# A fourth seven-product unit, low parts on GpSimd, and small transfers on SP's queue in an encoder block's gate/up stage

## Chip, core and metric

The kernel runs on one core of one Trainium2 chip. The metric is device microseconds of one execution, lower is better; the median of three runs is shown, and one more execution was profiled.

## The reference

One pre-norm encoder layer on a sequence of 256 rows, width 2048, everything in float32:

```
x = x + mix(rms_norm(x)) @ w_out            # four mixers: GLA, FNet, Hyena, short convolution
x = x + cross_attention(rms_norm(x), rms_norm(mem), w_xq, w_xkv, w_xo)
gate, up = split(rms_norm(x) @ w_gate_up)   # w_gate_up: 2048 x (2 * 5632)
x = x + (silu(gate) * up) @ w_down
return rms_norm(x)
```

Only the third line and the start of the fourth are touched by the change. The inputs that matter there are the 2048 x 11264 weight matrix, and 256 rows of normalised activations.

## The kernel before

**Precision by splitting.** TensorE multiplies float32r, which keeps fewer bits than float32. Each weight tile `raw` is therefore split into a high part `wh` (a cast on ScalarE, line 156) and a low part `wl = raw - wh` (a subtraction on VectorE, line 157); activations are split alike. A product is three matmuls (lines 495 to 497): high by high, high by low, low by high. One of these products is 128 rows of the sequence by 128 of the contraction by 512 columns.

**The weight stream.** Weights are laid out in HBM in the order of their use, in slabs of 16 blocks of 128 x 128 (1 MB, 128 x 2048). `Stream.raw` loads a slab on SP's queue (line 136) into one of three buffers, four in this stage; `Stream.make` splits a slab in parts of 1024 columns ahead of use, as long as `wh`/`wl` buffers are free: five parts in this stage.

**Plain slabs and units.** A plain slab of gate/up is two contraction tiles by two blocks of 512 columns; with two halves of the rows that is eight products. `seven(slab)` tells the slabs that are done as a *unit* instead: a Strassen-like form with seven products. For it the four blocks of the slab are first used as they are or replaced, in place, by sums and differences (line 189), and four parts are split: 512, 1024, 1024 and 1024 columns. The matching sums of activations are formed once, by `left()` (line 966), ahead of the first unit. The seven products of a unit partly go to four extra PSUM banks (p1, p5, p7, p6), into which all units of a pass add up.

**The loop.** `gate_up` (line 956) makes eleven passes over j. Each computes a block of 512 columns of gate and one of up: eight slabs i = 0 to 7. In pass 0 slab 5 is a unit, in passes 1 to 10 slabs 1, 3 and 5 (`sevens`, line 53). After the last unit `combine` (line 995) folds the four extra banks into SBUF tiles, starting with a copy of p1 (line 1000); the passes alternate between the two PSUM pools, so that the extra banks of one pass are the main ones of the next. After slab 7 `finish` (line 1009) adds the main banks, applies silu and the product, transposes the result on VectorE in blocks of 32 (line 525, into `u`) and stores it to HBM in `hidden` (line 530).

**Background work.** `combine`, `finish`, `turn`, `fetch` and `left` are generators that a planner (`Background`) steps between matmuls, by its own count of the work that VectorE owes (`bg.dve`). `turn` (line 1067) transposes the 16 residual tiles on VectorE, stores them to `xrows` and loads them back in row order (lines 1077, 1081); `fetch` (line 932) loads hidden tiles back and splits them for the next stage. In the stage described here, all of these transfers are issued on GpSimd's queue. The framework settles each engine's order by readiness, except where `keep_place` ties an instruction to the one before it; on its queue, each engine then issues strictly in that order.

**GpSimd's work.** Besides DMA issues it has a few memsets and one select at the kernel's start; it computes nothing in this stage.

Of the kernel before, what the change touches and what calls it, by code (L numbers as in the profile page):

```python
# [13 lines left out]
F32 = mybir.dt.float32  # L14
# [4 lines left out]
ALU = mybir.AluOpType  # L19
# [3 lines left out]
P = 128  # L23
R = 256
# [26 lines left out]
GU = 16 * (40 + 16 + 16 + 32 + 16)  # L51

def sevens(j):

    return (1, 3, 5) if j else (5,)


FORMED = 6
# [20 lines left out]
DOWN = GU // 16 + 16 * DFF // 1024  # L79
# [6 lines left out]
def seven(slab):  # L86

    j, i = divmod(slab - GU // 16, 8)
    return slab in UNITS if slab >= DOWN else j >= 0 and i in sevens(j)
# [22 lines left out]
class Stream:  # L112
# [34 lines left out]
                return pool  # L147
        return None

    def split(self, pool, at, r, edges):  # L150

        nc = self.nc
        wh, wl = (pool.tile([P, 1088], F32R, name=t, tag=t) for t in ("wh", "wl"))
        wh, wl = wh[:, at:at + 1024], wl[:, at:at + 1024]
        for a, b in zip(edges, edges[1:]):
            nc.scalar.copy(wh[:, a:b], r[:, a:b])  # L156
            nc.vector.tensor_tensor(out=wl[:, a:b], in0=r[:, a:b], in1=wh[:, a:b].bitcast(F32), op=ALU.subtract)  # L157
        self.bg.dve(edges[-1], len(edges) - 1)
        self.items.append((pool, wh, wl))

    def make(self):

        nc, (slab, part) = self.nc, self.todo
        n = 16 * slab + 8 * part
        if n >= NBLK - HELD:
            parts = [(self.places.pop(0)) for _ in range(2)]
            r = self.raw(slab)[:, part * 1024:part * 1024 + 1024]
            for a, (wh, wl) in zip((0, 512), parts):
                nc.scalar.copy(wh, r[:, a:a + 512])
                nc.vector.tensor_tensor(out=wl, in0=r[:, a:a + 512], in1=wh.bitcast(F32), op=ALU.subtract)  # L170
            self.bg.dve(1024, 2)
            self.items.append((None, parts))
            self.todo = (slab + part, 1 - part)
            return True
        pool = self.free(slab)
        if pool is None:
            return False
        raw = self.raw(slab)
        at = 48 if any(a <= n < b for a, b in ROWS) else 8
        r = raw[:, part % 2 * 1024:part % 2 * 1024 + 1024]  # L180
        if not seven(slab):
            mark = len(nc.cur_bb.bb.instructions)
            self.split(pool, at, r, [0, 256, 512, 1024] if n == 0 else [0, 512, 1024] if n == 8 else [0, 1024])
            if DOWN <= slab < DOWN + 2 * AHEAD:
                self.keep(mark)
            self.todo = (slab + part, 1 - part)
            return True
        mark = len(nc.cur_bb.bb.instructions)
        op = lambda out, a, b, what=ALU.subtract: nc.vector.tensor_tensor(out=out, in0=a, in1=b, op=what)  # L189
        self.split(pool, at, r, [0, 512] if part == 0 else [0, 1024])  # L190
        b11, b12, b22, b21 = (raw[:, a:a + 512] for a in range(0, 2048, 512))
        if part == 0:
            blk = raw.rearrange("p (b c) -> p b c", b=4)
            op(r.rearrange("p (b c) -> p b c", b=2), blk[:, 0:3:2, :], blk[:, 1:2, :].to_broadcast([P, 2, 512]))
            self.bg.dve(1024)
        elif part == 1:
            op(b22, b22, b11, ALU.add)
            op(b21, b21, b22)
            self.bg.dve(1024, 2)
        self.keep(mark)  # L200
        self.todo = (slab + part // 3, (part + 1) % 4)
        return True
# [87 lines left out]
class Block:  # L290
# [229 lines left out]
    def store_turned(self, to, u, src, keep=False):  # L520

        nc = self.nc
        self.bg.dve(src.shape[1])
        mark = self.mark()
        nc.vector.transpose(u, src)  # L525
        if keep:
            self.keep_place(mark)
        to = to.rearrange("(b f) t -> f b t", f=32)
        for a in range(4):
            nc.gpsimd.dma_start(to[:, :, 32 * a:32 * a + 32],  # L530
                                u[32 * a:32 * a + 32, :].rearrange("f (b t) -> f b t", t=32))


    def run(self):
# [237 lines left out]
    def attention(self):  # L772
        tc, nc, act, st = self.tc, self.nc, self.act, self.st
        with tc.tile_pool(name="atp", bufs=1) as atp, tc.tile_pool(name="kp", bufs=1) as kp, \
# [24 lines left out]
            def load_kv():  # L799
# [12 lines left out]
                for _ in range(5):  # L812
                    fetch()
# [118 lines left out]
    def fetch(self, f, ks, ahead, pause, form=None):  # L932

        m = {}
        for n in range(len(ks) + ahead):
            if n < len(ks):
                k = ks[n]
                while len(self.stored) <= k // 4:
                    yield
                m[k] = self.tmp()  # L940
                self.nc.gpsimd.dma_start(m[k], self.ff[k * P:(k + 1) * P, :])  # L941
            if n >= ahead:
                i = ks[n - ahead]
                if i >= PLAIN:
                    if i % 2:
                        form(i - 1, m.pop(i - 1), m.pop(i))
                        self.have += 2
                        yield 3.0
                    continue
                mark = self.mark()  # L950
                self.split(f[i], m.pop(i))
                self.keep_place(mark)
                self.have += 1
                yield pause

    def gate_up(self, sw, gp, f):

        nc, st = self.nc, self.st
# [6 lines left out]

        def left():

            for i in (5, 1, 3):
                t = [self.tmp() for _ in range(2)]
                for x, k in zip(t, (2 * i, 2 * i + 1)):  # L970
                    nc.scalar.activation(x, self.resk(k), AF.Copy, scale=self.gvec(V_NG + 32, k))
                (a11, a21), (a12, a22) = ((x[:, 0:P], x[:, P:R]) for x in t)
                s = gp.tile([P, 512], F32, name="u", tag="u", bufs=2)
                s1, s2, s3, s4 = (s[:, a:a + P] for a in range(0, 512, P))
                self.stt(s1, a21, -1.0, a22, ALU.mult, ALU.subtract)
                self.stt(s2, s1, -1.0, a11, ALU.mult, ALU.subtract)
                self.tt(s3, a11, a21, ALU.subtract)
                self.tt(s4, a12, s2, ALU.subtract)
                yield
                h, l = sums[i] = [sw.tile([P, 512], F32R, name=f"s{x}{i}") for x in "hl"]  # L980
                self.split2(h, l, s)
                yield
# [26 lines left out]
        def finish(j, cs, s):  # L1009

            for r in range(2):
                self.tt(s[r][0], cs[r][0], s[r][0], ALU.add)
                nc.scalar.activation(s[r][0], s[r][0], AF.Silu, scale=box["col"][:, r:r + 1])
                yield SOON
            for r in range(2):
                g, h = s[r]
                self.tt(h, cs[r][1], h, ALU.add)
                yield SOON
            for r in range(2):
                g, h = s[r]  # L1020
                u = gp.tile([P, 512], F32, name="u", tag="u", bufs=2)
                self.stt(h, h, box["col"][:, r:r + 1], g, ALU.mult, ALU.mult)
                yield SOON
                self.store_turned(self.ff[j * 512:(j + 1) * 512, r * P:(r + 1) * P], u, h)
                yield SOON
            self.stored.append(j)

        ready = [self.late, self.bg.add(norm())]
        forms = self.bg.add(left())
        turned = self.bg.add(self.turn())  # L1030
        early = end = None
        for j in range(DFF // 512):
# [5 lines left out]
            for i in range(8):  # L1038
# [18 lines left out]
                for k in (2 * i, 2 * i + 1):  # L1057
                    for c in range(2):
                        wh, wl = st.take("w_gate_up", k, cols[c], 4)
                        for r in range(2):  # L1060
                            self.part_rows(cs[r][c], r, self.h3[k], wh, wl, k == 0, k == KT - 1)
                            self.bg.poll()
            self.bg.drain(last)
            end = self.bg.add(finish(j, cs, s))
        return end, turned, early

    def turn(self):

        nc = self.nc
        to = self.xr.rearrange("(b t) f -> t b f", t=32)  # L1070
        for i in range(16):
            u = self.tmp()
            self.bg.dve(R)
            nc.vector.transpose(u, self.resk(i))
            for a in range(4):
                c = i * P + 32 * a
                nc.gpsimd.dma_start(to[:, :, c:c + 32], u[32 * a:32 * a + 32, :].rearrange("t (b f) -> t b f", f=32))  # L1077
            yield 4.0
        for c in range(4):
            for r in range(2):  # L1080
                nc.gpsimd.dma_start(self.half(c, r), self.xr[r * P:(r + 1) * P, c * 512:(c + 1) * 512])
            yield

    def half(self, c, r):
# [794 lines left out]
```

## Time and profile before

| | us |
|---|---|
| median of 3 runs | 1452.65 (1452.64 to 1453.78) |
| profiled execution | 1454.31 |
| its span, first to last instruction | 1452.4 |
| PE busy | 1439.1 |
| VectorE (DVE) busy | 1192.3 |
| ScalarE (ACT) busy | 844.1 |
| GpSimd (POOL) busy | 172.2 |

The granted TensorE clock was 0.998 of full speed on average. The passes of gate/up take from about 750 to 1208 us of the span. In rows that group instructions, the columns are line, engine, operation, written tile <- read tiles, shapes, count, then busy time, mean duration in ns and idle time before, with what ended it. In timelines, the first two columns are start and length in us, and xN is the number of instructions merged into the row. Matmul durations overlap, since the array is pipelined: the distance of two starts is what one matmul costs.

### The profile page before, as it was taken

Reading aid. Unit: us, or ns where it says so; the run is one execution under the profiler, and the core shown is the slowest. Engines: PE = TensorE matmul, PEld = TensorE weight load, DVE = VectorE, ACT = ScalarE, POOL = GpSimd, SP = SyncE. Lnnn points to the kernel's source line nnn. Section 1 sums busy time; section 2 is a strip of 40 time slices with the busy share of each in tenths; the row PEclk is TensorE's granted clock in tenths of the full one; section 3 lists DMA queues with packets and bytes.
Section 4 is the critical chain, followed back from the end, with each engine's and each line's share of the span. In section 5 each row is a group of like instructions: output and inputs, shape, how many; then the busy total and the mean of one; then the engine's idle time right before and its main releaser. Section 6 shows DMA issues by size and latency. Waiting matters only on the chain.

```text
span 1452.4 us, 19765 instructions
## 1 busy us (share of the span) xinstructions
PE 1439.1 (99%) x7231; PEld 1217.8 (84%) x7231; DVE 1192.3 (82%) x1750; ACT 844.1 (58%) x1254; POOL 172.2 (12%) x294
## 2 busy tenths in 40 slices
PE   9999999999999999999999999999999999999997
PEld 8888888898899888888888888888888888788886
DVE  6587768778868767877778999999999997988875
ACT  6565655466656646765565555555655564655554
POOL 0220100000000001100003334112111112100000
PEclk9999999999999999999999999999999999999999
DMA  9985654454535656555555767666667656655654
GB/s 352 339 289 197 220 193 168 152 187 156 195 129 206 215 179 224 172 170 195 178 205 205 277 234 243 220 209 237 233 220 250 221 200 220 214 184 199 225 203 146
DMA packets 57394, 307.17 MB, mean 211 GB/s; under 512 B 9773, under 2 KB 11470, under 8 KB 25680
## 3 DMA queue, kind: packets, MB, share of 16 engines
q1 hardware_dynamic: 45920, 281.11, 54.9%
q0 software_dynamic: 10944, 24.14, 5.4%
q8 instruction: 57, 0.93, 0.3%
q10 hardware_dynamic: 432, 0.66, 0.1%
q14 instruction: 41, 0.34, 0.1%
HBM read 291.71 MB, written 14.16 MB: 211 GB/s over the span
## 4 chain that ended last, share of the span: by engine, by line
PE 94%; DVE 2%; issue 2%; ACT 1%; DMA 1%; POOL 1%; SPq 0%; DVEq 0%; POOLq 0%; ACTq 0%
PE pg L444 19%; PE pg L496 13%; PE pg L497 13%; PE pg L495 13%; PE pg L445 10%; PE pm L496 6%; PE pm L495 6%; PE pm L497 6%; PE pm L1380 1%; DVE wl L157 1%; PE pg L441 1%; PE pg L442 1%; PE pm L895 1%; PE pm L868 1%; DMA tmp<-hidden 1%
## 5 line engine op out<-in xcount | busy, mean ns | idle before, releaser
L156 ACT CAST wh<-raw 128x1024 fp32r<-128x1024 f32 (+1 forms) x589 | 589.2, 1013 | 466.6 <-PE pg L497 149.7
L157 DVE TENSOR_TENSOR wl<-raw,wh 128x1024 fp32r<-128x1024 f32 (+1 forms) x589 | 681.4, 1175 | 177.8 <-ACT wh L156 171.7
L444 PE MATMUL pg<-act,wh 128*128 128x512 f32 x1104 | 387.5, 393 | 0.0
L445 PE MATMUL pg<-act,wl 128*128 128x256 f32 x1216 | 340.7, 280 | 0.0
L496 PE MATMUL pg<-wl,act 128*128 128x512 f32 (+1 forms) x689 | 268.3, 389 | 1.5 <-DVE wl L157 1.4
L495 PE MATMUL pg<-wh,act 128*128 128x512 f32 (+1 forms) x689 | 268.7, 391 | 0.0
L497 PE MATMUL pg<-wh,act 128*128 128x512 f32 (+1 forms) x689 | 268.3, 389 | 0.0
L444 PEld LDWEIGHTS pg<-act,wh 128*128 128x128 f32 x1104 | 207.4, 188 | 44.9
L445 PEld LDWEIGHTS pg<-act,wl 128*128 128x128 f32 x1216 | 228.5, 188 | 0.8 <-DVE wl L157 0.5
L496 PEld LDWEIGHTS pg<-wl,act 128*128 128x128 f32 x689 | 129.5, 188 | 29.6 <-DVE wl L157 3.1
L495 PEld LDWEIGHTS pg<-wh,act 128*128 128x128 f32 x689 | 129.6, 188 | 27.5 <-issue 0.8
L497 PEld LDWEIGHTS pg<-wh,act 128*128 128x128 f32 x689 | 129.4, 188 | 27.4 <-issue 0.4
L496 PE MATMUL pm<-wl,act 128*128 128x512 f32 x318 | 123.7, 389 | 0.0
L497 PE MATMUL pm<-wh,act 128*128 128x512 f32 x318 | 123.7, 389 | 0.0
L495 PE MATMUL pm<-wh,act 128*128 128x512 f32 x318 | 123.6, 389 | 0.0
L189 DVE TENSOR_TENSOR raw<-raw 128x1024 f32<-128x1024 f32 x129 | 111.7, 866 | 3.0
L530 POOL DMA_DIRECT2D hidden<-u x88 | 56.8, 653 | 162.3 <-DVE u L525 139.7
L495 PEld LDWEIGHTS pm<-wh,act 128*128 128x128 f32 x318 | 59.7, 188 | 12.5
L497 PEld LDWEIGHTS pm<-wh,act 128*128 128x128 f32 x318 | 59.7, 188 | 12.4
L496 PEld LDWEIGHTS pm<-wl,act 128*128 128x128 f32 x318 | 59.7, 188 | 12.4
L1077 POOL DMA_DIRECT2D xrows<-tmp x64 | 37.0, 586 | 182.7 <-DVE rc L323 126.6
L941 POOL DMA_DIRECT2D tmp<-hidden x44 | 24.5, 560 | 145.7 <-DVE f L319 73.4
(361 smaller groups left out, 1778.6 us busy)
## 6 DMA issues: line engine op xcount, KB each, us to landing
raw<-in_W SPq DMA_DIRECT2D x246, 1024.0 KB, 5.0
raw<-in_W SPq DMA_DIRECT2D x11, 512.0 KB, 7.5
hidden<-u POOLq DMA_DIRECT2D x88, 64.0 KB, 4.4
tmp<-hidden POOLq DMA_DIRECT2D x44, 128.0 KB, 4.6
res<-in_xT SPq DMA_DIRECT2D x8, 512.0 KB, 8.4
k<-in_mem SPq DMA_DIRECT2D x8, 256.0 KB, 6.8
k<-in_x SPq DMA_DIRECT2D x8, 256.0 KB, 9.9
keys<-k POOLq DMA_DIRECT2D x32, 64.0 KB, 5.4
```

Source lines behind the costliest of these rows:

```text
L156: nc.scalar.copy(wh[:, a:b], r[:, a:b])
L157: nc.vector.tensor_tensor(out=wl[:, a:b], in0=r[:, a:b], in1=wh[:, a:b].bitcast(F32), op=ALU.subtract)
L189: op = lambda out, a, b, what=ALU.subtract: nc.vector.tensor_tensor(out=out, in0=a, in1=b, op=what)
L441: self.nc.tensor.matmul(p[:, 0:R], wh, slot[:, 0:R], start=start, stop=False)
L444: self.nc.tensor.matmul(p[:, :], wh, slot[:, :], start=start, stop=False)
L445: self.nc.tensor.matmul(p[:, 0:R], wl, slot[:, 0:R], start=False, stop=stop)
L495: self.nc.tensor.matmul(p, hi, wh, start=start, stop=False)
L496: self.nc.tensor.matmul(p, hi, wl, start=False, stop=False)
L497: self.nc.tensor.matmul(p, lo, wh, start=False, stop=stop)
L530: nc.gpsimd.dma_start(to[:, :, 32 * a:32 * a + 32], u[32 * a:32 * a + 32, :].rearrange("f (b t) -> f b t", t=32))
L941: self.nc.gpsimd.dma_start(m[k], self.ff[k * P:(k + 1) * P, :])
L1077: nc.gpsimd.dma_start(to[:, :, c:c + 32], u[32 * a:32 * a + 32, :].rearrange("t (b f) -> t b f", f=32))
```

## The change

There are four edits.

1. `sevens(j)` returns (1, 3, 5, 6) for passes 1 to 10: slab 6 becomes a fourth unit, and `left()` forms the activation sums for it too. `combine` hence starts after slab 6.
2. In passes 1 to 10, the low part of the second half of each plain slab (now slabs 0, 2, 4, 7) is subtracted on GpSimd instead of VectorE, and is not counted in the planner's account of VectorE.
3. In `finish`, the stores of the transposed result go to SP's queue, and are emitted one planner step after the transposition. The early loads of `fetch` (those without a `form`) go to SP's queue too.
4. In `turn`, the stores go to SP's queue, emitted one step after their transposition; the loads back too.

```diff
 def sevens(j):
-    return (1, 3, 5) if j else (5,)
+    return (1, 3, 5, 6) if j else (5,)
...
-    def split(self, pool, at, r, edges):
+    def split(self, pool, at, r, edges, other=False):
...
             nc.scalar.copy(wh[:, a:b], r[:, a:b])
-            nc.vector.tensor_tensor(out=wl[:, a:b], in0=r[:, a:b], in1=wh[:, a:b].bitcast(F32), op=ALU.subtract)
-        self.bg.dve(edges[-1], len(edges) - 1)
+            (nc.gpsimd if other else nc.vector).tensor_tensor(out=wl[:, a:b], in0=r[:, a:b], in1=wh[:, a:b].bitcast(F32), op=ALU.subtract)
+        if not other:
+            self.bg.dve(edges[-1], len(edges) - 1)
...
-            self.split(pool, at, r, [0, 256, 512, 1024] if n == 0 else [0, 512, 1024] if n == 8 else [0, 1024])
+            self.split(pool, at, r, [0, 256, 512, 1024] if n == 0 else [0, 512, 1024] if n == 8 else [0, 1024],
+                       part == 1 and GU // 16 + 8 <= slab < DOWN)
...
+        self.put_turned(nc.gpsimd, to, u)
+
+    def put_turned(self, queue, to, u):
+
         to = to.rearrange("(b f) t -> f b t", f=32)
         for a in range(4):
-            nc.gpsimd.dma_start(to[:, :, 32 * a:32 * a + 32],
-                                u[32 * a:32 * a + 32, :].rearrange("f (b t) -> f b t", t=32))
+            queue.dma_start(to[:, :, 32 * a:32 * a + 32],
+                            u[32 * a:32 * a + 32, :].rearrange("f (b t) -> f b t", t=32))
...
-                self.nc.gpsimd.dma_start(m[k], self.ff[k * P:(k + 1) * P, :])
+                (self.nc.gpsimd if form else self.nc.sync).dma_start(m[k], self.ff[k * P:(k + 1) * P, :])
...
-            for i in (5, 1, 3):
+            for i in (5, 1, 3, 6):
...
                 yield SOON
-                self.store_turned(self.ff[j * 512:(j + 1) * 512, r * P:(r + 1) * P], u, h)
+                self.bg.dve(512)
+                nc.vector.transpose(u, h)
                 yield SOON
+                yield
+                self.put_turned(nc.sync, self.ff[j * 512:(j + 1) * 512, r * P:(r + 1) * P], u)
             self.stored.append(j)
...
-        for i in range(16):
-            u = self.tmp()
-            self.bg.dve(R)
-            nc.vector.transpose(u, self.resk(i))
-            for a in range(4):
-                c = i * P + 32 * a
-                nc.gpsimd.dma_start(to[:, :, c:c + 32], u[32 * a:32 * a + 32, :].rearrange("t (b f) -> t b f", f=32))
+        u = None
+        for i in range(17):
+            if u is not None:
+                for a in range(4):
+                    c = (i - 1) * P + 32 * a
+                    nc.sync.dma_start(to[:, :, c:c + 32], u[32 * a:32 * a + 32, :].rearrange("t (b f) -> t b f", f=32))
+            if i < 16:
+                u = self.tmp()
+                self.bg.dve(R)
+                nc.vector.transpose(u, self.resk(i))
             yield 4.0
         for c in range(4):
             for r in range(2):
-                nc.gpsimd.dma_start(self.half(c, r), self.xr[r * P:(r + 1) * P, c * 512:(c + 1) * 512])
+                nc.sync.dma_start(self.half(c, r), self.xr[r * P:(r + 1) * P, c * 512:(c + 1) * 512])
             yield
```

## The prediction

> **What bounds the kernel now.** I read first the page's busy times and slices, then the waits of the PE queue, then the busy times by stretch, then the timelines of PE and VectorE (DVE) around one pass of the gate/up loop.
>
> ```profile
> PE 1439.1 (99%) x7231; PEld 1217.8 (84%) x7231; DVE 1192.3 (82%) x1750; ACT 844.1 (58%) x1254; POOL 172.2 (12%) x294
> PE   9999999999999999999999999999999999999997
> DVE  6587768778868767877778999999999997988875
> POOL 0220100000000001100003334112111112100000
> PE pg L496 <- DVE wl L157: 1.9, 2, 1.4
> core 0: us, PE busy (x) PEld busy (x) DVE busy (x) ACT busy (x) POOL busy (x), PEclk, DMA share, GB/s
> 700.00:779.50 79.50, 79.50 (x422) 68.39 (x421) 60.26 (x107) 45.46 (x70) 14.98 (x26) 1.00 0.56 189
> 779.50:1194.30 414.80, 414.80 (x1832) 343.47 (x1831) 394.99 (x455) 235.82 (x266) 91.71 (x150) 1.00 0.66 231
> ```
>
> PE is busy 99% of the span and its longest kind of wait adds up to 1.9 us, so the kernel ends when PE has done its matmuls. The gate/up stretch is special: DVE stands at 9 there too. The next rows measure one pass (one value of j: two column blocks of 512, eight slabs).
>
> ```profile
> L1000 ACT COPY g<-pm x6: 578/578/579, 779.5 to 1194.3; 128x512 f32<-128x512 f32 x6
> 948.07 0.39 PE L495 MATMUL pg<-wh,act 128*128 128x512 f32 x1
> 958.95 0.39 PE L495 MATMUL pm<-wh,act 128*128 128x512 f32 x1
> ```
>
> The copy that opens each pass's recombination runs 11 times, so ten passes take 1194.3 - 779.5 = 414.8 us, 41.48 each. Between the two PE rows lie two plain slabs, 48 matmuls, in 10.88 us: 0.2267 us each, whatever the 0.39 of their pipelined durations says. A pass has five plain slabs (24 matmuls) and three units of seven products (21): 183 x 0.2267 = 41.49. So the pass is PE's without a gap, and DVE is busy 394.99 / 10 = 39.5 of it: 2.0 us spare. That spare is what the change lives on.
>
> **The fourth unit.** In passes 1 to 10 slab 6 becomes a unit: 3 matmuls fewer, 0.68 us a pass, **-6.8 us in all**, if PE stays the bound. Its price is on DVE:
>
> ```profile
> 1104.37 1.23 DVE L189 TENSOR_TENSOR raw<-raw 128x1024 f32<-128x1024 f32 x1
> 1105.51 1.22 DVE L157 TENSOR_TENSOR wl<-raw,wh 128x1024 fp32r<-128x1024 f32 x1
> 1106.76 1.42 DVE L189 TENSOR_TENSOR raw<-raw 128x512 f32<-128x512 f32 x2
> 1108.10 0.42 DVE L319 TENSOR_TENSOR f<-tmp,f 128x256 fp32r<-128x256 f32 x1
> 1108.43 6.89 DVE L157 TENSOR_TENSOR wl<-raw,wh 128x1024 fp32r<-128x1024 f32 x6
> 1120.28 0.69 DVE L157 TENSOR_TENSOR wl<-raw,wh 128x512 fp32r<-128x512 f32 x1
> 1121.01 1.23 DVE L189 TENSOR_TENSOR raw<-raw 128x1024 f32<-128x1024 f32 x1
> ```
>
> Starts, not durations, give the occupancy: a low part of 1024 columns holds DVE (6.89 - 1.22) / 5 = 1.14 us, one of 512 0.73, the 1024-wide difference 1.14, the pair of 512-wide ones 1.34. A plain slab costs 2 x 1.14 = 2.28, a unit 3 x 1.14 + 0.73 + 1.14 + 1.34 = 6.63: +4.35 a pass. ACT gets 1.5 casts of about 1 us more and is busy 235.82 of 414.80, so it hides them. The one more set of sums formed ahead of pass 0's unit (four 128-wide operations and a split, some 3 us) falls where DVE has 79.50 - 60.26 = 19 us idle; without that cover it costs those 3 us.
>
> **Four low parts to GpSimd.** The second half of each plain slab of passes 1 to 10, four a pass after the change, leaves DVE: -4 x 1.14 = -4.56. So DVE goes from 39.5 to 39.3 of a pass that PE would do in 180 x 0.2267 = 40.80: spare 1.5 us. GpSimd computes nothing in the trace that is like it. Its nearest rows:
>
> ```profile
> masks.py:199 POOL TENSOR_SCALAR_AFFINE_SELECT ident<-ident 128x128 f32<-128x128 f32 x1 | 0.3, 287 | 0.1
> L1858 POOL MEMSET const-float32-1.0<- 128x1 f32 x1 | 0.1, 108 | 0.0
> L530 POOL DMA_DIRECT2D hidden<-u x88 | 56.8, 653 | 162.3 <-DVE u L525 139.7 <-PE pm L497 22.0 <-issue 0.4
> ```
>
> One operand read costs (287 - 108) / 127 = 1.41 ns an element, so 1024 columns take at least 0.11 + 1.44 = 1.55 us; a second operand at worst as much again, 2.99. I take the middle, 2.27: 9.1 us of GpSimd a pass. That time alone delays nobody: GpSimd is idle otherwise, and PE reads a part some 8 us after it is made (below).
>
> The Trainium skill (GPSIMD Engine Reference, section 3.1) gives 4497 ns for a two-input operation of 2048 columns; by estimate 2.25 us for 1024, and the sum would be the same; no run here shows it.
>
> What decides is whether DVE stands still meanwhile. Below, DVE's one-tensor transposition, its PSUM operation and its two-SBUF-operand operation of 512 columns all start about 0.6 us apart, so DVE's second operand comes over a read path that is already used at full rate. In the trace GpSimd only generates descriptors beside that (L530), which stretches no DVE operation, and its one tensor read happens before DVE has work. So the price of one such GpSimd operation to DVE is bounded by 0 and by its whole length. I take the whole: two operands of 1024 columns have to be read somewhere, and DVE's path has no free slots to share. It is an inference, and both ends stay in the range.
>
> ```profile
> 1124.77 0.68 DVE L319 TENSOR_TENSOR g<-pg,g 128x512 f32<-128x512 f32 x1
> 1125.37 0.68 DVE L189 TENSOR_TENSOR raw<-raw 128x512 f32<-128x512 f32 x1
> 1125.97 0.68 DVE L319 TENSOR_TENSOR h<-pg,h 128x512 f32<-128x512 f32 x1
> L525 DVE STREAM_TRANSPOSE u<-h 128x512 f32<-128x512 f32 x18 | 11.7, 686 | 0.0
> 949.89 1.22 DVE L157 TENSOR_TENSOR wl<-raw,wh 128x1024 fp32r<-128x1024 f32 x1
> ```
>
> DVE operations with at most one SBUF tensor (eight on PSUM, two transpositions a pass, 10 x 0.6 = 6.0 of 39.3 us, 15%) would go on beside GpSimd. So a pass costs DVE 39.3 + 9.1 x 0.85 = 47.0 us, 6.2 more than PE's 40.80. Ten passes: 62 us, less the lead that DVE has when it begins: the row at 949.89 is the low part of the slab whose first matmul is the PE row at 958.95, ready at 951.1, 8 us ahead. **+54 us.**
>
> The Trainium skill (SBUF — State Buffer, "Who interferes with whom") says that a DVE instruction with two SBUF inputs and a GpSimd instruction that reads SBUF exclude each other for a whole instruction; this is the full price, while without the rule the sum would be that of the first rival; no run here shows it yet.
>
> **Stores and loads to SP.** Eight stores a pass, 64 small stores, 8 loads back, 16 early loads leave GpSimd, whose queue then holds only the low parts: nothing of theirs waits behind a store. On SP they sit among the weight loads.
>
> ```profile
> L136 SPq DMA_DIRECT2D raw<-in_W x72: 327/328/328, 822.6 to 1193.9; - x72
> DMA to landing us min/median/max: 4.8/5.1/8.2
> 964.25 0.33 SPq L136 DMA_DIRECT2D raw<-in_W  x1
> 965.46 1.30 DVE L525 STREAM_TRANSPOSE u<-h 128x512 f32<-128x512 f32 x2
> 969.02 0.33 SPq L136 DMA_DIRECT2D raw<-in_W  x1
> 983.85 3.18 ACT L156 CAST wh<-raw 128x1024 fp32r<-128x1024 f32 x3 [1.54 <-DVE raw L189]
> ```
>
> SP issues in 0.33 us and otherwise waits. The transpositions of a pass, at 965.5 to 966.8, fall between two weight loads; the later, of 969.02, is cast at 985.0 (the second of the casts at 983.85): 16 us, of which landing takes 5. Eight stores in between, 8 x 0.33 = 2.6 us, are hidden by the 11 left; if they wait for a late transposition, all weight loads behind them wait too, and ACT's casts, DVE's and GpSimd's parts after that. I take 0; above the cover it costs what the wait exceeds 11 us, below nothing it cannot go, since no engine on the path waits for these stores in time.
>
> **Sum.** Against the profiled execution (span 1452.4 us, 1.9 more around it: 1454.31): 1454.31 - 6.8 + 54 = 1501.5. It ran 1.66 us above the median of the runs, 1452.65, so the forecast in their terms is **1500 us**. With GpSimd at 1.55 us a part: 39.3 + 6.2 x 0.85 = 44.6, 3.8 x 10 - 8 = 30, 1476; at 2.99: 49.5, 79, 1525.
>
> **Rivals.** *No interference* (faster). DVE 39.3 under 40.80, PE stays the bound: 1452.65 - 6.8 = **1446**. For it: L530's descriptors beside DVE disturb nothing. Against: they are not tensor reads. It flips to slower when a GpSimd part costs DVE more than (41.48 - 39.3) / 4 = 0.55 us, a quarter of its length, before the lead is counted. *Partial interference*: half the length, 9.1 / 2 x 0.85 = 3.9, DVE 43.2, 2.4 x 10 - 8 = 16: **1462**. *The banks come late*. The recombination now starts after slab 6, not 5.
>
> ```profile
> 953.36 0.68 DVE L319 TENSOR_TENSOR h<-pm,g 128x512 f32<-128x512 f32 x1
> ```
>
> Its last read of the old banks ends at 954.04; that bank is first written two products (6 matmuls, 1.36 us) after 958.95, so 6.3 us are spare, and a slab later (5.44 us) 0.8. Two more low parts in front of it on DVE (2.28 us) would make PE wait 1.5 us a pass: 15 - 6.8 = +8, **1461**; it eats the gain at 1.5 us of delay, and with a little less the time is unchanged. For it: units in slabs 5 and 6 follow each other, DVE's densest work. Against: the planner drains these steps before the next pass.
>
> **How the numbers follow.** Full interference 0.48 (1476 to 1525); partial 0.15; banks late 0.10 (slower), or just late enough to cancel the gain 0.04; no interference 0.23. A measurement tells 0.2%, 2.9 us, from no change. Faster 0.23; same 0.07, with 0.03 from partial interference that the lead swallows; slower 0.70. The range reaches from just under the clean case, 1445, to a GpSimd part of some 2.6 us, 1512; about 0.15 is left out, mostly longer parts. The likeliest case alone: 1476 to 1525.
>
> **What would show it.** Right: in the passes DVE nearly 100% busy or idle "for POOL", its low parts or their gaps stretched beside GpSimd's, passes of 46 to 47 us between the copies of p1, PE waiting for DVE's or GpSimd's low parts; GpSimd parts of 2 to 2.5 us. Wrong: passes of 40.8 us with PE without a gap (no interference); PE waiting at a pass's start behind the recombination (banks); ACT's casts waiting for weight loads (SP).

## The result, and the profile after

| | before | after |
|---|---|---|
| median of 4 runs, us | 1452.94 | 1532.94 (1531.01 to 1533.42) |
| ratio, 95% interval | | 1.0547 (1.0529 to 1.0565) |
| profiled execution, us | 1454.31 | 1531.01 |
| its span, us | 1452.4 | 1529.2 |

The change makes the kernel 80 us slower. That is the direction of the forecast, but 33 us more than its 1500, and above its range. From the page after, its busy times and three of its slice rows:

```profile
PE 1460.7 (96%) x7201; PEld 1217.2 (80%) x7201; DVE 1261.5 (82%) x1765; ACT 855.7 (56%) x1277; POOL 175.3 (11%) x158
PE   9999999999999999999998998999888897999997
DVE  6687769779678678777789999999999996888885
POOL 0221000000000001100012122221222221200000
```

PE has 30 matmuls fewer, as intended (7231 to 7201), and yet falls from 99% to 96%. The holes lie in slices 22 to 34, and up to 33 DVE stands at 9 and POOL computes beside it. Slice 34 is a hole of its own kind: DVE falls to 6 there.

To divide the loss I use marks that don't depend on another engine: the first matmul of pass 1 (the 4370th in every trace) and the first one behind pass 10 (the 1032nd from the end). Ten passes lie between them. The stretch of after by busy times (columns as in the prediction: PE, PEld, DVE, ACT, POOL, granted clock, DMA share, GB/s):

```profile
793.45:1273.98 480.53, 434.18 (x1802) 342.07 (x1800) 458.90 (x457) 245.14 (x283) 111.29 (x44) 0.97 0.59 190
```

In before the marks are at 793.03 and 1207.83, the same 414.80 us as between the copies. So of the 76.8 us by which the span grew, **65.7 lie in the ten passes** (480.53 - 414.80), **10.7 behind them** (1529.2 - 1273.98 = 255.2, against 1452.4 - 1207.83 = 244.6), and 0.4 ahead.

**In the passes.** What PE waits for there (four of eight rows; total, times, longest):

```profile
PE pg L498 <- DVE wl L157: 16.6, 14, 2.4
PE pm L498 <- DVE wl L157: 16.1, 13, 2.2
PE pg L497 <- DVE g L321: 3.2, 3, 1.5
PE pm L497 <- ACT wh L156: 2.9, 4, 1.2
```

The low parts from DVE come late: 32.7 us of the 46.3 that PE idles (480.53 - 434.18). PE's busy time has grown as well, although it has fewer matmuls (434.18 against 414.80): the granted clock is 0.97 here, which the last section comes back to. The groups of DVE in the window from 850 to 1250 say which of its operations grew:

```profile
L157 DVE TENSOR_TENSOR wl<-raw,wh 128x1024 fp32r<-128x1024 f32 x133 | 197.3, 1502 | 14.0 <-ACT wh L156 12.8
L191 DVE TENSOR_TENSOR raw<-raw 128x512 f32<-128x512 f32 x66 | 45.4, 687 | 1.5
L191 DVE TENSOR_TENSOR raw<-raw 128x1024 f32<-128x1024 f32 x33 | 40.0, 1212 | 0.6
L157 DVE TENSOR_TENSOR wl<-raw,wh 128x512 fp32r<-128x512 f32 x33 | 34.0, 1031 | 2.2 <-ACT wh L156 2.0
L325 DVE SCALAR_TENSOR_TENSOR h<-h,rc,g 128x512 f32<-128x512 f32 x17 | 19.6, 1181 | 1.1 <-ACT g L1019 1.1
L1031 DVE STREAM_TRANSPOSE u<-h 128x512 f32<-128x512 f32 x18 | 11.6, 682 | 0.0
L321 DVE TENSOR_TENSOR g<-pg,g 128x512 f32<-128x512 f32 x8 | 5.4, 681 | 0.0
L157 POOL TENSOR_TENSOR wl<-raw,wh 128x1024 fp32r<-128x1024 f32 x40 | 111.2, 2783 | 519.8 <-ACT wh L156 489.0
```

The last row is GpSimd's, from the page: a low part takes it 2.78 us (2.42 to 3.44). The low parts grew: 1.22 to 1.50 us on average, 0.69 to 1.03. So did the product `h<-h,rc,g`, which also reads two SBUF tensors (`rc` is one column). The transposition and the operation that takes one tensor from PSUM kept their 0.68. The differences of the units (L191) read two SBUF tensors and kept their 0.69 and 1.21, but of the 120 in this stage only one runs beside a subtraction. The records from 790 to 1310 us, sorted by whether a subtraction ran at the same time, say it more sharply (mean us, and how many):

| operation of DVE | SBUF tensors read | no subtraction running | beside a subtraction |
|---|---|---|---|
| low part, 1024 columns | 2 | 1.22 (123) | 2.15 (47) |
| low part, 512 columns | 2 | 0.68 (31) | 2.68 (9) |
| product `h<-h,rc,g` | 2 | 0.74 (11) | 1.42 (11) |
| transposition `u<-h` | 1 | 0.68 (11) | 0.68 (11) |

How that looks in the timeline of both engines:

```profile
1023.90 6.08 POOL L157 TENSOR_TENSOR wl<-raw,wh 128x1024 fp32r<-128x1024 f32 x2 [14.56 <-ACT wh L156]
1024.84 2.86 DVE L157 TENSOR_TENSOR wl<-raw,wh 128x1024 fp32r<-128x1024 f32 x1
1027.61 0.68 DVE L321 TENSOR_TENSOR h<-pg,m 128x512 f32<-128x512 f32 x1
1028.21 2.05 DVE L321 TENSOR_TENSOR act<-tmp,act 128x256 fp32r<-128x256 f32 x1
1030.18 0.68 DVE L157 TENSOR_TENSOR wl<-raw,wh 128x512 fp32r<-128x512 f32 x1
```

GpSimd makes two low parts in 6.08 us. DVE's low part, 1.22 us when alone, is issued into the first and takes 2.86. The PSUM operation after it goes on at full speed beside the second. The operation on two SBUF tensors of 256 columns, 0.42 us when alone, ends 0.28 us after GpSimd's second part does (1023.90 + 6.08 = 1029.98). GpSimd is held up in the same way. The five subtractions that began with no two-tensor operation of DVE under way took 2.42 to 2.44 us; one that began 0.42 us before such an operation's end took 2.70, and one that began 1.16 us before it 3.44, in both cases 2.28 us more than DVE still had to run. This is exclusion rather than sharing.

**Behind the passes.** 9.5 of the 10.7 us are one wait. Rows of PE, ACT and SP's queue:

```profile
1299.95 1.22 PE L497 MATMUL pm<-wh,f 128*128 128x512 f32 x2 [9.49 <-ACT wh L156]
1298.86 1.99 ACT L156 CAST wh<-raw 128x1024 fp32r<-128x1024 f32 x2 [7.03 <-DMA raw<-in_W]
1260.52 7.17 SPq L136 DMA_DIRECT2D raw<-in_W  x2
1267.74 6.08 SPq L1085 DMA_DIRECT2D xrows<-tmp  x10
1273.87 1.87 SPq L1093 DMA_DIRECT2D res<-xrows  x4
1282.89 4.40 SPq L536 DMA_DIRECT2D hidden<-u  x8
1287.34 1.95 SPq L1093 DMA_DIRECT2D res<-xrows  x4
1289.38 2.91 SPq L136 DMA_DIRECT2D raw<-in_W  x3
```

PE waits for a cast, the cast for a weight load, and the weight load stands on SP behind 26 moved transfers. From 1267.7 to 1289.4 SP issues no weights at all. For 7.1 us of that it issues nothing: the last pass's eight stores wait for their transposition, and everything queued behind them waits too:

```profile
SPq L536 <- DVE u L1031: 7.1, 1, 7.1
```

### The profile page after: what moved, and what is told of

The parts are those of the page before. It is cut to its first block, busy times and chain, and to the rows that moved or that the text cites. A ratio compares the mean times of both kernels' runs of the same rounds, so it can differ in the third digit from the quotient of the medians.

```text
span 1529.2 us, 19825 instructions
## 1 busy us (share of the span) xinstructions
PE 1460.7 (96%) x7201; PEld 1217.2 (80%) x7201; DVE 1261.5 (82%) x1765; ACT 855.7 (56%) x1277; POOL 175.3 (11%) x158
## 2 busy tenths in 40 slices
DMA packets 118449, 307.16 MB, mean 201 GB/s; under 512 B 71213, under 2 KB 74958, under 8 KB 86736
## 4 chain that ended last, share of the span: by engine, by line
PE 75%; DVE 13%; issue 6%; ACT 2%; DMA 1%; POOL 1%; SPq 0%; ACTq 0%; DVEq 0%; POOLq 0%
PE pg L446 18%; PE pg L498 10%; PE pg L499 10%; PE pg L497 10%; PE pg L447 10%; DVE wl L157 8%; PE pm L498 4%; PE pm L499 4%; PE pm L497 3%; DVE raw L191 2%; ACT wh L156 2%; PE pm L1392 1%; POOL tmp L947 1%; PE pg L443 1%; PE pg L444 1%
## 5 line engine op out<-in xcount | busy, mean ns | idle before, releaser
L156 ACT CAST wh<-raw 128x1024 fp32r<-128x1024 f32 (+1 forms) x609 | 600.5, 1006 | 524.1 <-PE pg L499 157.3
L157 DVE TENSOR_TENSOR wl<-raw,wh 128x1024 fp32r<-128x1024 f32 (+2 forms) x569 | 716.0, 1274 | 188.5 <-ACT wh L156 182.0
L497 PE MATMUL pg<-wh,act 128*128 128x512 f32 (+1 forms) x664 | 258.2, 395 | 5.5 <-DVE g L321 3.2
L499 PE MATMUL pg<-wh,act 128*128 128x512 f32 (+1 forms) x664 | 260.1, 392 | 0.0
L157 POOL TENSOR_TENSOR wl<-raw,wh 128x1024 fp32r<-128x1024 f32 x40 | 111.2, 2783 | 519.8 <-ACT wh L156 489.0
L498 PEld LDWEIGHTS pg<-wl,act 128*128 128x128 f32 x664 | 126.1, 190 | 38.7 <-DVE wl L157 12.6
L497 PEld LDWEIGHTS pg<-wh,act 128*128 128x128 f32 x664 | 125.7, 189 | 35.6 <-DVE g L321 4.4
L499 PEld LDWEIGHTS pg<-wh,act 128*128 128x128 f32 x664 | 125.9, 190 | 26.6 <-issue 0.4
L191 DVE TENSOR_TENSOR raw<-raw 128x1024 f32<-128x1024 f32 x159 | 137.4, 864 | 3.5
L497 PE MATMUL pm<-wh,act 128*128 128x512 f32 x293 | 113.1, 396 | 3.3 <-DVE g L321 3.1
L499 PE MATMUL pm<-wh,act 128*128 128x512 f32 x293 | 116.2, 396 | 0.0
L497 PEld LDWEIGHTS pm<-wh,act 128*128 128x128 f32 x293 | 55.8, 191 | 17.1 <-DVE g L321 3.9
L499 PEld LDWEIGHTS pm<-wh,act 128*128 128x128 f32 x293 | 56.3, 192 | 11.8
L498 PE MATMUL pg<-wl,sh 128*128 128x512 f32 x81 | 33.3, 411 | 10.1 <-DVE wl L157 10.1
L498 PE MATMUL pm<-wl,sh 128*128 128x512 f32 x83 | 34.2, 412 | 7.8 <-DVE wl L157 7.8
```

Of the source, the lines that this page charges most:

```text
L157: (nc.gpsimd if other else nc.vector).tensor_tensor(out=wl[:, a:b], in0=r[:, a:b], in1=wh[:, a:b].bitcast(F32), op=ALU.subtract)
L497: self.nc.tensor.matmul(p, hi, wh, start=start, stop=False)
L498: self.nc.tensor.matmul(p, hi, wl, start=False, stop=False)
L499: self.nc.tensor.matmul(p, lo, wh, start=False, stop=stop)
```

## The experiments

All kernels differ from after, or from before, by the lines shown. "Each pass" is a tenth of the time between the two marks, "rest" what comes behind them; both are of the profiled execution.

| kernel | units | GpSimd's 1024-column operations | transfers on | median, us | ratio (95%) | each pass | rest |
|---|---|---|---|---|---|---|---|
| before | 3 | none | GpSimd | 1452.94 | | 41.48 | 244.6 |
| after | 4 | 40 subtractions | SP | 1532.94 | 1.0547 (1.0529 to 1.0565) | 48.05 | 255.2 |
| e1_memset | 4 | 40 zero fills | SP | 1465.50 | 1.0079 (1.0064 to 1.0094) | 41.66 | 253.3 |
| e2_no_gpsimd | 4 | none | SP | 1481.28 | 1.0192 (1.0177 to 1.0207) | 43.65 | 249.1 |
| e3_sp_alone | 3 | none | SP | 1465.90 | 1.0085 (1.0070 to 1.0100) | 42.25 | 246.3 |
| e4_three_units | 3 | 50 subtractions | SP | 1496.11 | 1.0293 (1.0275 to 1.0310) | 45.37 | 245.6 |
| e5_copy | 4 | 40 copies | SP | 1470.98 | 1.0121 (1.0104 to 1.0138) | 42.29 | 253.1 |
| e6_gpsimd_queue | 4 | 40 subtractions | GpSimd | 1551.14 | 1.0674 (1.0658 to 1.0690) | 51.11 | 246.8 |
| e7_half | 4 | 20 subtractions | SP | 1502.60 | 1.0335 (1.0321 to 1.0349) | 45.67 | 251.1 |
| e8_memset_gpsimd_queue | 4 | 40 zero fills | GpSimd | 1466.11 | 1.0092 (1.0076 to 1.0107) | 42.57 | 245.8 |
| e9_last_stores | 3 | none | SP, last stores GpSimd | 1460.07 | 1.0047 (1.0032 to 1.0062) | 42.25 | 243.2 |
| e10_three_passes | 4 in 3 passes | none | GpSimd | 1457.06 | 1.0021 (1.0012 to 1.0030) | 41.71 | 244.3 |
| e11_unit_alone | 4 | none | GpSimd | 1479.73 | 1.0177 (1.0163 to 1.0191) | 43.75 | 245.5 |

### Is it what GpSimd reads?

**e1_memset.** GpSimd writes zeros in place of its 40 low parts, and reads nothing.

```diff
-            (nc.gpsimd if other else nc.vector).tensor_tensor(out=wl[:, a:b], in0=r[:, a:b], in1=wh[:, a:b].bitcast(F32), op=ALU.subtract)
+            if other:
+                nc.gpsimd.memset(wl[:, a:b].bitcast(F32), 0.0)
+            else:
+                nc.vector.tensor_tensor(out=wl[:, a:b], in0=r[:, a:b], in1=wh[:, a:b].bitcast(F32), op=ALU.subtract)
```

> The changed kernel, except that GpSimd's 40 operations fill the low parts with zeros instead of subtracting (so those low parts are left out of the product); as many of them, in the same place of the order, but they read nothing from SBUF. Theory A (a GpSimd operation that reads SBUF holds up VectorE's operations with two SBUF operands): VectorE's low parts of 1024 columns are back at 1.22 us each throughout, a pass is 40.8 us, TensorE has no gaps in the passes; what is left of the 10 us wait for weights at the end of the stage may remain: 1446 to 1458 us. Theory B (the 4.6 times more small packets and the stores on SP's queue slow VectorE's operands or the weight stream): these stay, so 1515 to 1535 us. Theory C (the fourth unit is dearer on VectorE than worked out): VectorE bound still, above 1480 us.

1465.5 us: 67 us of the loss are gone, and the theories that needed more than 1480 fall. It is 7.5 over the first theory's range, though. Busy times of its ten passes, and its rows of GpSimd and DVE (from 829.9 to 1201.4):

```profile
794.36:1210.91 416.55, 412.56 (x1802) 336.44 (x1800) 390.52 (x459) 246.44 (x283) 40.54 (x45) 1.00 0.66 219
L158 POOL MEMSET wl<- 128x1024 f32 x35 | 33.5, 957 | 328.9 <-PE pm L501 150.0 <-PE pg L501 149.2 <-DVE g L324 23.5
L160 DVE TENSOR_TENSOR wl<-raw,wh 128x1024 fp32r<-128x1024 f32 x141 | 169.5, 1218 | 15.0 <-ACT wh L156 13.6
```

DVE's low parts are back at 1.22 us, those that run beside a fill included (30 of them, 1.22 us). As many operations of DVE (459 against 457) hold it 390.52 us where after has 458.90: 68.4 us of stretch, **1.71 us for each of the 40 subtractions**. What is left of the loss lies mostly behind the passes: 253.3 against before's 244.6, with a wait of PE for a cast of 7.9 us, as in after.

**e5_copy.** GpSimd copies the raw tile into the low part instead: one operand read, one written.

```diff
-                nc.gpsimd.memset(wl[:, a:b].bitcast(F32), 0.0)
+                nc.gpsimd.tensor_copy(wl[:, a:b], r[:, a:b])
```

The line taken out is e1's.

> The changed kernel, except that GpSimd's 40 operations copy raw into the low part (one SBUF operand read, no subtraction, so that the product is another one). Theory A (any GpSimd operation that reads SBUF holds up VectorE's two-operand operations for about as long as it runs): a copy takes at least 1.55 us by the select at the kernel's start; at 1.0 to 1.8 us of holding up per operation the time lies between the zero fill (1465.5) and the subtraction (1532.9), 1490 to 1520 us, with single VectorE operations stretched by up to a whole copy. Rival (only two operands read at once by GpSimd collide): VectorE's low parts stay at 1.22 us and the time at 1465.

1470.98 us, below the first theory's range and above the other's. Its rows, from 780 to 1210:

```profile
L158 POOL CAST wl<-raw 128x1024 fp32r<-128x1024 f32 x40 | 57.5, 1438 | 506.6 <-PE pg L501 335.4 <-PE pm L501 171.2
L160 DVE TENSOR_TENSOR wl<-raw,wh 128x1024 fp32r<-128x1024 f32 x164 | 210.5, 1302 | 14.6 <-ACT wh L156 13.6
```

A copy does hold DVE's low parts (1.30 us on average), but little: its passes have DVE busy for 404.64 us, (404.64 - 390.52) / 40 = 0.35 us a copy. The copy is half as long, and since it doesn't need the cast it starts at other moments (it waits for PE to free the buffer, not for ACT). The trace shows the same exclusion on a smaller scale: the nine copies that began with no two-tensor operation of DVE under way took 1.04 to 1.05 us, and most of the longer ones 0.91 us more than DVE still had to run. So a copy keeps DVE's next such operation out for 0.91 us at most, a subtraction for 2.28; and 23 operations of DVE are stretched here, 39 in after. How much each of the two saves was not separated.

**e7_half.** Only slabs 0 and 4 of a pass give their second half to GpSimd: 20 subtractions.

```diff
-                       part == 1 and GU // 16 + 8 <= slab < DOWN)
+                       part == 1 and GU // 16 + 8 <= slab < DOWN and (slab - GU // 16) % 8 in (0, 4))
```

> The changed kernel with 20 instead of 40 low parts on GpSimd (plain slabs 0 and 4; those of slabs 2 and 7 on VectorE). Theory A (each operation on GpSimd costs more than it takes off VectorE): from none on GpSimd (1481.3) to 40 (1532.9) it is 51.6 us, 1.3 us an operation, so 20 of them give some 1507 us, 1495 to 1520. Rival (a threshold: GpSimd's parts come late only when they follow each other closely): at or below 1481 us.

1502.6 us, within the first theory's range. **e2_no_gpsimd** gives none (the condition is `False`).

> The changed kernel with all low parts on VectorE: fourth unit and transfers on SP's queue stay. Theory A: VectorE has 39.5 + 4.35 = 43.9 us of work in a pass that TensorE would do in 40.8, nothing stretched: ten passes of 3.1 us more, less some 4 us of lead, less 6.8, plus up to 10 us of waiting for weights at the stage's end: 1470 to 1490 us, so leaving GpSimd out is faster than using it by 40 us or more. Theory B (packets and SP's queue): 1520 us or more. Theory C (unit dearer): 1500 us or more.

1481.28 us, as expected. With after these two make a series of 0, 20 and 40 subtractions: 1481.3, 1502.6, 1532.9. Each subtraction taken from DVE frees 1.14 us there, and yet each *costs* the kernel 1.07 us for the first 20 and 1.52 for the next. By the passes: e2 takes 43.65 us; less the low parts moved, DVE would need 43.65 - 2 x 1.14 = 41.4 in e7 and 39.1 in after; measured 45.67 and 48.05. So **one subtraction on GpSimd takes 2.15 to 2.24 us from a pass** that DVE bounds, about twice what it frees. (In after the lower clock may have a part in it; e7's clock was 1.00.)

**e4_three_units** has the change without the fourth unit: five plain slabs, five subtractions a pass.

```diff
-    return (1, 3, 5, 6) if j else (5,)
+    return (1, 3, 5) if j else (5,)
...
-            for i in (5, 1, 3, 6):
+            for i in (5, 1, 3):
```

> The changed kernel with three units: five low parts of a pass on GpSimd, transfers on SP's queue. Theory A: VectorE has 39.5 - 5 x 1.14 = 33.8 us of work a pass plus 5 x 1.78 us of being held up (what the changed kernel shows per GpSimd operation) = 42.7, with the 2 us of idling that the changed kernel has in each pass 44.7, against TensorE's 41.5: 1465 to 1490 us; the stretch of VectorE's two-operand operations beside GpSimd as in the changed kernel. Theory C (the fourth unit is what costs): no more than 1464 us, since VectorE has 33.8 us of its own work only.

1496.11 us, 6 over the first theory's range, far above the 1464 of the other. Against e3, the same kernel without the subtractions, they cost 30.2 us, although DVE had 2.0 us to spare in a pass. The loss isn't even: passes 1 to 5 take 45.5 to 50.3 us, passes 6 to 10 only 41.5 to 42.6, with five subtractions in each. So a subtraction has no fixed price; why the later passes escape is open.

### The transfers

**e3_sp_alone.** Only the stores and loads move to SP: e4's edit and the condition `False`.

> Only the transfers on SP's queue: three units, all low parts on VectorE. Theory A: VectorE's operations unstretched and TensorE the bound in the passes; only the wait for weights at the end of the stage can show: 1452 to 1464 us, and if the wait of the changed kernel comes from SP's order alone, some 10 us of it: 1462. Theory B: most of the 80 us, above 1500 us.

1465.90 us, 1.9 over the first theory's range and 12.6 over before in the same comparison (1453.31); the prediction had put 0. 7.7 us are lost in the passes, 1.8 behind them, 1.7 ahead. Rows of SP's queue and of ACT in one pass:

```profile
L536 SPq DMA_DIRECT2D hidden<-u x80: 303/492/1846, 802.0 to 1189.3; - x80
970.00 4.70 SPq L536 DMA_DIRECT2D hidden<-u  x8
975.36 0.38 SPq L136 DMA_DIRECT2D raw<-in_W  x1
986.55 1.05 ACT L156 CAST wh<-raw 128x1024 fp32r<-128x1024 f32 x1 [1.51 <-DVE raw L191]
988.32 0.59 ACT L1006 COPY g<-pg 128x512 f32<-128x512 f32 x1 [0.72 <-PE pg L499]
988.80 4.84 ACT L156 CAST wh<-raw 128x1024 fp32r<-128x1024 f32 x5
```

A store is issued in 0.49 us, not in a weight load's 0.33. The weight load that before issued at 969.02 goes out at 975.36; since this pass itself starts 2.6 us later than in before (961.56 against 958.95), it is 3.7 us late within its pass. Its data would still be there in time: the cast at 988.80 waits for no DMA. But ACT's order is fixed by readiness when the program is built, and here the cast stands behind the copy of p1, which waits for PE, while in before it ran ahead of that copy. It starts 27.25 us into the pass instead of 26.08, and the low parts after it are late in turn. ACT waits for PE ahead of this copy ten times out of eleven (10.3 us in all), in before never. That the later load is what turned the order round is inferred. The moved transfers also go out in many more small packets (71213 under 512 B, 9773 in before), but in the passes a weight load still lands in 5.4 us (median; 5.1 in before), so that is not where the time goes.

**e9_last_stores.** e3, with the eight stores of pass 10 back on GpSimd.

```diff
-                self.put_turned(nc.sync, self.ff[j * 512:(j + 1) * 512, r * P:(r + 1) * P], u)
+                self.put_turned(nc.gpsimd if j == 10 else nc.sync, self.ff[j * 512:(j + 1) * 512, r * P:(r + 1) * P], u)
```

> Transfers alone on SP's queue (three units, no low part on GpSimd), but the eight stores of the last pass on GpSimd's queue. Theory: some 5 us of the 12.6 us that transfers alone cost come from three weight loads that queue behind the last pass's stores on SP (issued at 1226.7 to 1228.0 us instead of 1202.7 to 1218.6): these are issued earlier again and the time falls to 1458 to 1462 us. Rival (all of it comes from the stores within the passes): unchanged, 1465 to 1467 us.

1460.07 us, as expected: 5.8 less than e3 by the medians, 3.2 of it in the rest of the profiled executions (246.3 to 243.2); the passes stayed at 42.25. At the stage's end these stores hold up weight loads that have nothing to hide behind.

**e6_gpsimd_queue.** The other way round: before with the fourth unit and the 40 subtractions, the transfers left on GpSimd's queue.

> Fourth unit and low parts on GpSimd as in the change, but all transfers on GpSimd's queue as in the kernel before. Theory A with a separate price of 12.6 us for the transfers on SP's queue (transfers alone: 1465.9): 1515 to 1525 us. Rival (the move to SP is what keeps GpSimd's low parts from waiting behind stores that wait for VectorE's transpositions): slower than the change, 1540 us or more, with GpSimd waiting for VectorE's transpositions ahead of low parts.

1551.14 us, not the 1515 to 1525 of the first theory but what the rival expected (1540 or more): with the subtractions, the move to SP *saves* 18.2 us. The rest is 246.8, 8.4 less than in after, so most of the loss at the stage's end is absent, but a pass takes 51.11. One place:

```profile
855.71 6.72 DVE L191 TENSOR_TENSOR raw<-raw 128x512 f32<-128x512 f32 x2
856.48 4.66 POOL L157 TENSOR_TENSOR wl<-raw,wh 128x1024 fp32r<-128x1024 f32 x2
```

DVE's pair of differences, 1.42 us in before, takes 6.72: it is held through two subtractions that follow each other at once, without getting in between (in after's timeline above, DVE did get in between two). Subtractions that wait behind stores come in such pairs (under 0.5 us between them), 10 here and 5 in after. Six DVE operations in e6 take over 3.6 us, none in after.

### The fourth unit

**e11_unit_alone.** Before with `sevens` and `left()` of the change, and nothing else.

> The kernel before with the fourth unit alone: all low parts on VectorE, transfers on GpSimd's queue. Theory: VectorE has 39.5 + 4.35 = 43.9 us in a pass of 40.8 on TensorE, 31 us over ten passes less 4 us of lead and less 6.8: 1453 + 20 = 1473; if the transfers on SP's queue add the same 12.6 us with and without the fourth unit, 1481.3 - 12.6 = 1469. So 1466 to 1476 us. Rival (VectorE catches up, TensorE stays the bound): 1446 to 1453 us.

1479.73 us, 26 over before and 4 over my range. Its ten passes, and PE's longest waits in them:

```profile
794.79:1232.28 437.49, 419.15 (x1802) 334.27 (x1800) 430.15 (x498) 243.26 (x283) 93.19 (x153) 1.00 0.62 214
PE pg L496 <- DVE wl L157: 6.8, 7, 1.4
PE pm L496 <- DVE wl L157: 5.4, 5, 1.4
```

DVE is busy for 43.0 of 43.75 us a pass, 0.8 less than the prediction's 39.5 + 4.35 = 43.85. I had taken a lead off; what is left of it in ten passes is 1 us: they take 22.7 us more than in before (437.49 - 414.80), where 10 x (43.85 - 40.80) - 6.8 = 23.7 would come without any. The first pass does profit, with 41.24 us; from the second on none is under 42.5. The trace of before shows why there is so little: in the pass from 958.95, the last low part of slab 3 is made from 975.80 to 977.02, and PE's first matmul on it starts at 978.21, 1.2 us later. Over the ten passes of before the low parts are ready 1.0 to 9.6 us ahead; the 8 us of the prediction belong to the first part of a pass, near the upper end.

**e10_three_passes** asks for that lead directly: the unit in passes 4, 7 and 10 only, with two passes between to recover.

```diff
-    return (1, 3, 5) if j else (5,)
+    return (1, 3, 5, 6) if j in (4, 7, 10) else (1, 3, 5) if j else (5,)
```

> The kernel before with a fourth unit in passes 4, 7 and 10 only, all low parts on VectorE, transfers on GpSimd's queue: 3 x 4.35 = 13 us more VectorE work spread over passes that leave it 2.0 us each. If VectorE's spare time carries it, 3 x 0.68 = 2.0 us faster: 1450 to 1451.5 us against 1452.6 to 1453.5 before. If the lead of some 4 to 8 us isn't enough within a pass, TensorE waits 2 us or so in each of these passes: 1453 to 1458 us.

1457.06 us, 3.3 over before. Pass 4 itself does run at PE's 40.80 us, but the pass behind it takes 42.70 and the one behind pass 7 43.23, where before has 41.48: even at one such pass in three, the debt costs more than the unit saves.

**e8_memset_gpsimd_queue** is the rival of the prediction in pure form: unit, zero fills, transfers where they were. DVE has the 39.1 us a pass that the prediction wanted, GpSimd reads nothing.

> Fourth unit, GpSimd's operations filling zeros (40 low parts left out), transfers on GpSimd's queue: neither SBUF reads of GpSimd nor transfers on SP. If these two are all that costs, the 6.8 us of the fourth unit show: 1446 to 1449 us. If the recombination a slab later makes TensorE wait for banks, each pass starts with a gap: 1450 to 1462 us.

1466.11 us, not 1446 to 1449, and above the 1450 to 1462 for a gap at each pass's start as well. The rest is 245.8, so it is lost in the passes, where PE waits for a little of everything (three of six rows):

```profile
792.83:1218.52 425.69, 413.91 (x1802) 335.85 (x1800) 391.34 (x460) 247.44 (x284) 126.21 (x185) 1.00 0.64 220
PE pg L500 <- ACT wh L156: 2.8, 3, 1.7
PE pm L501 <- DVE wl L160: 2.4, 2, 1.2
PE pm L501 <- POOL wl L158: 2.0, 1, 2.0
```

DVE idles for 34 us and still comes late. What DVE and ACT wait for in the same stretch:

```profile
DVE wl L160 <- ACT wh L156: 22.3, 28, 2.3
ACT wh L156 <- DVE raw L194: 74.4, 45, 3.3
```

DVE's low parts wait for ACT's casts, more than twice as long as in before (9.4 us in its ten passes), and ACT's casts of a unit for DVE's differences, which in before took nearly as long (69.6 us) without harm; some fills stand on GpSimd's queue behind stores (the 2.0 us of PE). In e1, without the stores on that queue, a pass takes 41.66, still 0.86 over PE's 40.80. Which order of the instructions would remove these waits was not tried.

## Why the prediction was right and wrong

**Right: the direction and its mechanism.** The prediction took the whole holding-up of DVE by GpSimd's reads, on an inference from PSUM and SBUF operations that start at the same distance. Those rows alone could not tell exclusion from sharing; the runs do: 68.4 us of stretch against zero fills, on operations with two SBUF tensors only. The price came out about right, too, partly by luck: forecast 9.1 x 0.85 = 7.7 us of DVE a pass, measured 6.84, because a share that was too high met a part that was too short.

The Trainium skill (SBUF — State Buffer, "Who interferes with whom") says that a VectorE instruction with two SBUF inputs contends with a GpSimd instruction that reads SBUF, and not with one that only writes. The traces agree on both: DVE's low part takes 2.15 us on average beside a subtraction, 1.22 beside a fill. A copy reads too, and so contends by that rule; here it cost 0.35 us.

**A term with a wrong size: GpSimd's part.** Forecast 2.27 us, measured 2.78, with a minimum of 2.42: what a part takes over that is GpSimd held up by DVE's operations in turn. The lower end of 1.55 was no bound either, since a copy of 1024 columns took 1.04 us at the least: the whole difference between a select of 128 columns and a fill of one had been put down to the operand read, although a fill of 128 columns already takes 0.20 us of the 0.29. The Trainium skill (GPSIMD Engine Reference, section 3.1) has 4497 ns for 2048 columns, by estimate 2.25 for 1024; the trace's minimum is 7% above that.

**Wrong: the range.** The forecast of 47.2 us net in the passes fell 18.5 short of 65.7, and that of 0 behind them 10.7 short. Three steps failed.

*"Less the lead that DVE has when it begins", 8 us.* It was read as a stock that ten passes could use up. After's first pass takes 47.7 us already (from its first matmul to the 180th after it), e11 keeps 1 us of a lead in ten passes, and e10 loses with one in three. The low part that is ready 8 us ahead is the first of its pass; the latest of a pass are ready 1.0 to 1.5 us ahead. This is 8 of the 18.5 us.

*"A pass costs DVE 47.0", as if it were busy all the time.* Measured: 39.05 (e1) + 6.84 (stretch) = 45.9 busy, but 48.05 long. DVE idles 2.16 us a pass, mostly for casts by ACT:

```profile
DVE wl L157 <- ACT wh L156: 15.6, 17, 1.7
```

A bound whose engine has to wait for others in a loop is not reached; in e1 and e8, where PE should be the bound, 0.9 and 1.8 us a pass are missing in the same way. This idling, 21.6 us in ten passes, less the 11 by which the busy time was put too high, is the other 10.5 us. How much of it comes of the halved clock (last section) is open.

*Stores and loads on SP, "I take 0".* Alone they cost 12.6 us (e3). The cover of 11 us held for the data and not for ACT's order; and it was read in mid-stage, while the cost in the change lies at the stage's end (9.5 us), where `turn`'s stores, its loads and the last stores come together. The prediction did name that wait ("all weight loads behind them wait too") and gave it no price.

**The rivals.** *No interference* at 1446 had 0.23; e8 shows that it was not to be had even without reads by GpSimd (1466), and with the transfers on SP 1465.5 (e1). Its sum took PE for the bound as soon as DVE's busy time lay under PE's. The dividing line was wrong for the same reason: DVE needs more than 1.5 us of spare. *Partial interference*: a subtraction held DVE for 1.71 of its 2.78 us, 61% where the forecast had 85% of 2.27, or 1.93. The share was nearer to this rival, the price to the forecast, since the part was longer; and this rival's 1462 took the same lead off. *The banks come late*: PE's waits for `g` and `h` are 8.4 us in after, none in e1, which has the same late recombination; so that alone doesn't make PE wait, and in after the waits go with DVE being late. The range missed because the three steps add up on one side: each was taken at its cheap end.

**What is settled, and what isn't.** The fourth unit, the subtractions and the transfers each lose by themselves: +26 (e11), +30 (e4 less e3), +12.6 (e3). They don't add: with the unit there, moving the transfers costs 1.6 more (e2 against e11), and with the subtractions it saves 18.2. Open are the uneven price in e4, what the clock adds in after, and the last 17 us of e8. No version here beats before.

## What to carry to other kernels

Before moving work from VectorE to GpSimd, look at what both read: where the moved operation reads SBUF and VectorE's own work has two SBUF inputs, price it as VectorE's time as well. Here a two-input subtraction freed 1.14 us and took 2.2 from a pass; a copy held VectorE for 0.35, and a fill not at all. Busy time under the bound's is not yet spare: in a loop of engines that feed each other, 0.9 to 1.8 us of 41 were lost to waits even with 1.7 to spare (e1, e8), so an exchange of TensorE time for VectorE time must leave more than that. Before putting stores on the queue that feeds the weights, look at the end of the stage and at the order of the engine behind the loads, not only at the time to landing in the middle.

## What the runs showed of the hardware that I had not expected

- A GpSimd operation that only writes leaves VectorE alone: 1.22 us for the low part beside fills of 0.957 us.
- Holding up goes both ways: a subtraction that begins while VectorE is at a two-tensor operation lasts some 2.28 us longer than that operation still runs (2.42 us at the least, up to 3.44).
- VectorE may not get in between two GpSimd operations that follow at once: 6.72 us for a pair of 512-column differences that takes 1.42.
- The same 64 KB store takes 0.49 us to issue on SP, against 0.33 for a 1 MB weight load.
- The granted TensorE clock was 1.00 in the passes of most kernels, 0.98 in e4, 0.97 in after and 0.94 in e6. In after it stands at 0.50 in six stretches of 3.4 or 6.8 us, 27.3 us in all, which is 13.6 us of PE's time. Each begins 1.3 to 3.8 us behind the last matmul before a hole in which PE's starts are at least 2.2 us apart; but two such holes (at 949.2 and 1191.5) are followed by none. So the waits come first and the clock follows. Passes with such a stretch take 47.7 to 51.9 us, the four without 44.0 to 47.3. DVE is also busy for longer in them (45.3 to 50.1 against 42.4 to 44.8), so how much the clock adds to a pass is not shown.
